# Page order and buffers in a decoder-layer step: keys of the third pair ahead of the first pair's values, a score buffer that pages may share

## The chip, the core and the metric

One core of one Trainium2 chip. The metric is the device time of one execution of the whole program in microseconds. The kernel before took 876.76 us (median of three runs, 876.49 to 877.36).

## What is computed

One decoder layer for 256 prompt tokens and for 8 decode requests of 8 tokens each (64 sample tokens), so 320 tokens stand side by side. Cut to what matters:

```
z = x @ w_in                                  # 2048 -> 8272 columns, all 320 tokens
A: index scores -> top-k keys; sparse attention over 8 heads x 128
   prompt: over its own 256 keys; sample: over 2048 cached keys in 16 pages of 128, and its 8 new keys
   s = q . K[selected] * 128**-0.5 ; p = softmax(s) ; a = p @ V[selected]
B: HGRN2 gated recurrence, 4 heads
M: cross-attention, 4 heads: prompt over 256 memory rows (mk, mv = mem @ w_mem), sample over cached memory
cat = [a, b, m] * silu(gates) ;  y = cat @ w_out ;  x <- LayerNorm(2**0.25 * x + y)
```

The selection is made by a mask: the sample's attention reads all 2048 cached keys and values of every request (`page_table` names the pages), and the mask takes the keys that are not selected out of the softmax. Outputs are the layer's result, the new keys and values, states and memory keys and values.

## The kernel before, in words

**Matmuls.** Inputs are split into a high and a low part in a fast matmul type (xh, xl for activations; wh, wl for weights), and three products (high x high, low x high, high x low) stand for one. A projection block gives 128 columns for 320 tokens (tile pj, matmuls of 128x320); its weights come in two halves of 512 KB, loaded to one of three raw buffers wr, split by ScalarE (wh) and VectorE or GpSimd (wl). `PROJECTIONS` (line 30) lists the order; the memory keys and values (mem: 16 steps, each of a 512 KB weight tile and a 128 KB activation tile) stand late in it, then mq, g3 and g2. After the last projection `split` (line 1474) writes the concatenated branch outputs as high and low parts over xh and xl, and the output projection (pieces named wo) begins.

**Pages.** The sample's attention works on pairs of requests. `PAGES` (line 31) is the order of the page work: K2 are the keys of the third pair, V0 the values of the first, XK and XV the cached memory keys and values. Each K or V entry is eight units, an X entry one unit; a unit reads two tiles of two pages (4 x 512 KB). `unit` (line 657) issues its matmuls, which use the array as four strips of 32 columns. K units write scores to S[p] (a buffer of tag S, 2048 + 64 columns); `soft` (line 1110) adds the mask, takes the exponential and transposes to PTt[p] (one buffer, so it waits until the values of pair p - 1 are done); V units multiply PTt[p] by value pages into the PSUM tile va. The first softmax needs the top-k selection, a long run of VectorE work.

**What sets the order.** Every engine's instructions are put in order when the program is built. `Plan` (line 56) keeps an estimated clock per engine; the main loop (line 1958) steps along it: `loads` (line 1901) issues transfers from SyncE's queue (weights first, then stores, then pages), then come weight splitting, evictions and background generators (`background`, line 1865: index scores, softmax, recurrence, cross-attention, `split`), and at last either page units (`units_now`, line 733) or one quantum of a projection. A visit is one run of page units on TensorE: two units together when both are loaded, one unit alone when the next weights are not about to be ready, or after a wait of 9 us by the plan's clock (`PATIENCE`). On the chip each engine runs its list in order and waits on semaphores.

**Buffers.** `BUFS` (line 236) gives six buffers of tag pg (8 KB per partition) and two of tag S. Pages go to pg; so do other tiles for a time (indexer queries q, relu results more, half of the indexer's cached keys ci, the final LayerNorm's data, the split weights kept for the output projection's last chunk). A page load is issued when a pg buffer is free or about to be, at most two units ahead of the unit that is next, with less than 8 us of transfers outstanding by the plan's clock. `page` (line 637) loads a page's number from SBUF to a register of SyncE just before the transfer that uses it, with bounds given.

```
31   PAGES = ["K0", "K1", "V0", "K2", "V1", "V2", "K3", "XK0", "XK1", "XV0", "XV1", "V3"]
1924 if (half > 46 and n < len(punits) and len(PG) + ("q" in st) + ("more" in st) + ci_live(0) < BUFS["pg"] and n <= nunit + 2
1925         and plan.slot_free("pg", BUFS["pg"]) <= plan.now + 0.2 and plan.t["DMA"] < plan.now + 8):
1926     load_pages(n, b)
```

The record of nearly every instruction goes through one helper (line 154), so that the profile names all of them by that line; groups are told apart by their tiles. The functions that the change touches:

Of the kernel before, what the change touches and what calls it, by code (L numbers as in the profile page):

```python
# [27 lines left out]
PAST = 2048  # L28
HALF = 1032
PROJECTIONS = ["ikw", "iq", "aq", "ak", "av", "b0", "b1", "g0", "b2", "g1", "b3", "mem", "mq", "g3", "g2"]  # L30
PAGES = ["K0", "K1", "V0", "K2", "V1", "V2", "K3", "XK0", "XK1", "XV0", "XV1", "V3"]
# [14 lines left out]
IDLE = 3.0  # L46
TABLES = {AF.Exp: "exp_ln", AF.Ln: "exp_ln", AF.Silu: "silu", AF.Sqrt: "sqrt"}
# [95 lines left out]
class Engine:  # L143
# [3 lines left out]
    def __getattr__(self, op):  # L147
# [3 lines left out]
        def call(*a, **k):  # L151
# [9 lines left out]
            if op == "value_load":  # L161
                plan.t[eng] = max(plan.t[eng], plan.now) + 0.65
            elif op == "dma_start":
                plan.dma(eng, outs[0], ins[0])
            elif op == "indirect_dma_start":
                plan.dma(eng, k["out"], k["in_"])
            elif outs:
                n = max(math.prod(x.shape[1:]) for x in outs + ins)
                plan.run(eng, self.cost(op, outs, ins, n), outs, ins,
                         op in PORT and all(x.space != bass.MemoryType.PSUM for x in outs + ins))  # L170
# [55 lines left out]
def hymba_step(ctx: ExitStack, tc: tile.TileContext, I, O):  # L226
# [9 lines left out]
    BUFS = {"t": 17, "s8": 10, "pg": 6, "bp": 2, "wr": 3, "wh": 4, "wl": 4, "S": 2, "row": 4, "mA": 2, "mB": 2, "pj": 2}  # L236
# [355 lines left out]
    def prep(i, j):  # L592
# [9 lines left out]
        if s.get("res") and kept.index(i) < HOMES:  # L602
            if not spare_w:
                for cols, tag in ((2880, "cat0"), (2240, "cat1"), (2320, "PT"), (2048, "pg"), (2048, "pg")):
                    t = new([128, cols], tag, F32R)
                    plan.split.add(t.tensor.name)
                    spare_w.extend(t[:, 512 * k:512 * k + 512] for k in range(4))
# [29 lines left out]
    def page(e):  # L637
        return SP.value_load(ptab[0:1, e:e + 1], min_val=0, max_val=159)

    def load_pages(n, b):  # L640
        kind, p, u = punits[n]
        t = new([128, 2, 1024], "pg")
        PG[n, b] = t
        for j in range(2):
            if kind in ("XK", "XV"):
                SP.dma_start(t[:, j, :], I["c" + kind][4 * p + 2 * b + j])
            else:
                e = (2 * p + b) * 16 + 2 * u + j
                SP.dma_start(t[:, j, :], I["c" + kind.lower()][bass.ds(page(e), 1)].rearrange("o p c -> p (o c)"))
# [7 lines left out]
    def unit(n):  # L657
        kind, p, u = punits[n]
        tl = [PG.pop((n, b)) for b in range(2)]
        if kind == "K":  # L660
            if u == 0:
                S[p] = new([128, PAST + NS], "S")
            if u % 2 == 0:
# [48 lines left out]
    def unit_ready(n):  # L712
# [3 lines left out]
        if kind == "K":  # L716
            return u % 2 or ("aq", 7) in done and plan.slot_free("kv", 1) <= plan.now and (
                u or plan.slot_free("S", BUFS["S"]) <= plan.now and len(S) + ci_live(1) < BUFS["S"]
# [51 lines left out]
    def ci_live(k):  # L770
        return sum([0, 1, 0, 1][p] == k and ("ci", p) in st for p in range(4))

    def idx_load():
# [3 lines left out]
        for sp in range(2):  # L777
            for p in (2 * sp, 2 * sp + 1):
                st["ci", p] = x = new([128, PAST], ("pg", "S")[p % 2])
# [68 lines left out]
    def idx_sample():  # L848
# [44 lines left out]
        def stack(k):  # L893
# [12 lines left out]
            if (c, f) == (1, 0):  # L906
                del st["ci", 2 * sp + a]
# [202 lines left out]
    def soft(p):  # L1110
# [35 lines left out]
        ACT.copy(PTt[p][:, 16, :], ps)  # L1146
        del S[p]
# [56 lines left out]
    def cross_prompt(h):  # L1204
        yield from wait("mem", ("mq", h), "attn")
        yield from room(4)
# [6 lines left out]
        DVE.tensor_scalar(s8[:, 2:4], s8[:, 0:2], -QS, None, op0=OP.mult)  # L1213
        P = [T(256), T(256)]
        pts = [T(256), T(256)]
        free(MQ.pop(h), st["mkT"][h])
# [12 lines left out]
        free(*P)  # L1229
        for nt in range(2):  # L1230
# [670 lines left out]
    def loads():  # L1901
        nonlocal nw, npg
        while True:
# [20 lines left out]
            if (half > 46 and n < len(punits) and len(PG) + ("q" in st) + ("more" in st) + ci_live(0) < BUFS["pg"] and n <= nunit + 2  # L1924
                    and plan.slot_free("pg", BUFS["pg"]) <= plan.now + 0.2 and plan.t["DMA"] < plan.now + 8):
# [7 lines left out]
            if n == len(punits) and nunit == n and half > n_in - 6 and ("r", 2) not in st:  # L1933
                ln_load(2)
                continue
            return
# [177 lines left out]
```

## Time and profile before

| | us |
|---|---|
| median of three runs | 876.76 |
| the profiled execution, its own time | 878.17 |
| its span, first to last instruction | 876.4 |
| TensorE busy | 860.5 (98%) |
| VectorE busy | 558.0 (64%) |
| ScalarE busy | 423.0 (48%) |
| GpSimd busy | 311.7 (36%) |
| moved by DMA | 266.55 MB, mean 304 GB/s |

How to read it: the profile is one execution. Engines are PE (TensorE), PEld (its weight loads, beside the matmuls), DVE (VectorE), ACT (ScalarE), POOL (GpSimd) and SP (SyncE, which only issues transfers here; SPq is its queue). A group is written `out<-in` with tile names; "x128" counts instructions. A row of the windows gives, for one stretch, the busy microseconds of PE, PEld, DVE, ACT and POOL with counts, then the granted share of TensorE's clock, the busy share of the DMA engines and GB/s. A row of the timeline is start, duration, engine, line, operation, and in brackets the idle time before it and what ended that. A list of waits gives total, number and longest in us. Matmuls are pipelined and their ends are modelled, so the distance between starts tells more than the busy time.

### The profile page before, as it was taken

The numbers are of one execution on the slowest core, as the hardware profiler recorded it, in microseconds if no ns is written. First come the engines' busy times: TensorE is split into PE (matmuls) and PEld (weight loads), VectorE is DVE, ScalarE is ACT, GpSimd is POOL, SyncE is SP. The second block draws the span as 40 slices with busy tenths as digits, with TensorE's granted clock in tenths as the row PEclk, the third lists the DMA queues.
The fourth block names the chain that finished last, engine by engine and source line by source line (L and its number), as shares of the span: only waits on it lengthen the run. The fifth ranks groups of instructions, "written<-read, shape, count | busy, mean of one in ns | idle before, by whom it ended". The sixth has DMA issues, their size and how long they took to land.

```text
span 876.4 us, 19974 instructions
## 1 busy us (share of the span) xinstructions
PE 860.5 (98%) x6972; PEld 730.7 (83%) x6974; DVE 558.0 (64%) x1128; ACT 423.0 (48%) x909; POOL 311.7 (36%) x310
## 2 busy tenths in 40 slices
PE   9999999999999999999999999999999999999996
PEld 8999898878988998879888786777888878788885
DVE  6778989748789984645745563585444333943655
ACT  6445666545463444435545364444444433744432
POOL 0543562255644461322433142334222000613424
PEclk9999999999999999999999999999999999999999
DMA  8555544899999975999999999999998999876633
GB/s 309 182 165 160 158 144 146 300 342 405 362 410 337 372 260 161 339 411 354 398 367 399 412 377 401 405 347 383 325 408 331 350 384 384 295 269 200 192 101 120
DMA packets 84375, 266.55 MB, mean 304 GB/s; under 512 B 10609, under 2 KB 21810, under 8 KB 83634
## 3 DMA queue, kind: packets, MB, share of 16 engines
q1 hardware_dynamic: 83250, 263.18, 81.3%
q0 software_dynamic: 1024, 2.10, 0.8%
q8 instruction: 55, 0.90, 0.4%
q14 instruction: 46, 0.38, 0.1%
HBM read 256.50 MB, written 8.73 MB: 303 GB/s over the span
## 4 chain that ended last, share of the span: by engine, by line
PE 91%; DMA 3%; DVE 2%; ACT 1%; SPq 1%; issue 1%; DVEq 0%; ACTq 0%
PE pj L154 53%; PE mB L154 11%; PE va L154 10%; PE mA L154 9%; PE kv L154 7%; DMA pg<-in_ck 2%; SPq L154 1%; ACT wh L154 1%; DVE wl L154 1%; DMA pg<-in_xT 1%; DVE t L154 1%; DMA wr<-in_wt 0%; DVE pg L154 0%; ACT t L154 0%; DVE cat L154 0%
## 5 line engine op out<-in xcount | busy, mean ns | idle before, releaser
L154 PE MATMUL pj<-xh,wh 128*128 128x320 f32 x1008 | 321.9, 319 | 0.0
L154 PE MATMUL pj<-xh,wl 128*128 128x320 f32 x1008 | 311.5, 309 | 0.0
L154 PE MATMUL pj<-xl,wh 128*128 128x320 f32 x1008 | 311.3, 309 | 0.0
L154 ACT CAST wh<-wr 128x512 fp32r<-128x512 f32 x338 | 205.4, 618 | 210.9 <-PE pj L154 155.3
L154 DVE TENSOR_TENSOR wl<-wr,wh 128x512 fp32r<-128x512 f32 x231 | 178.2, 785 | 183.1 <-ACT wh L154 180.2
L154 POOL TENSOR_TENSOR wl<-wr,wh 128x512 fp32r<-128x512 f32 x107 | 145.2, 1362 | 296.8 <-ACT wh L154 272.9
L154 PEld LDWEIGHTS pj<-xh,wh 128*128 128x128 f32 x1008 | 189.4, 188 | 18.4 <-issue 12.7
L154 PEld LDWEIGHTS pj<-xl,wh 128*128 128x128 f32 x1008 | 189.5, 188 | 1.3
L154 PEld LDWEIGHTS pj<-xh,wl 128*128 128x128 f32 x1008 | 189.2, 188 | 0.0
L154 POOL TENSOR_TENSOR t<-t,t 128x320 f32<-128x320 f32 (+3 forms) x44 | 41.1, 935 | 88.5 <-DVE t L154 41.2
L154 PE MATMUL kv<-pg,qpad 128*32 128x256 f32 x1032 | 62.7, 380 | 3.4 <-DMA pg<-in_ck 3.4
L154 PE MATMUL va<-pg,PT 128*32 128x512 f32 x512 | 59.6, 596 | 0.0
L154 PEld LDWEIGHTS kv<-pg,qpad 128*32 128x32 f32 x1032 | 33.4, 110 | 27.2 <-issue 5.7
L154 PEld LDWEIGHTS va<-pg,PT 128*32 128x32 f32 x512 | 15.1, 109 | 30.5 <-issue 29.3
L154 DVE MAX8 PT<-PT 128x8 f32<-128x1032 f32 x32 | 39.5, 1234 | 0.5
L154 DVE MATCH_REPLACE8 PT<-PT 128x1032 f32<-128x1032 f32 x32 | 39.0, 1217 | 0.0
L154 ACT ACTIVATE t<-t 128x320 f32<-128x320 f32 (+1 forms) x44 | 18.5, 455 | 24.7 <-DVE t L154 24.4
L154 POOL TENSOR_TENSOR t<-t,tabm 128x320 f32<-128x320 f32 x16 | 14.0, 878 | 39.1 <-DVE t L154 35.4
L154 POOL DMA_INDIRECT pg<-in_ci,row x16 | 16.6, 1040 | 26.8 <-DVE row L154 19.9
L154 DVE TENSOR_TENSOR t<-t,t 128x320 f32<-128x320 f32 (+4 forms) x28 | 17.6, 629 | 13.4 <-ACT t L154 6.9
L154 ACT ACTIVATE S<-kv 128x512 f32<-128x512 f32 x16 | 9.6, 598 | 32.6 <-PE kv L154 32.6
L154 PE MATMUL mB<-t,wh 128*128 128x256 f32 x128 | 24.0, 286 | 0.0
(360 smaller groups left out, 1314.1 us busy)
## 6 DMA issues: line engine op xcount, KB each, us to landing
pg<-in_ck SPq DMA_DIRECT2D x128, 512.0 KB
pg<-in_cv SPq DMA_DIRECT2D x128, 512.0 KB
wr<-in_wt SPq DMA_DIRECT2D x126, 512.0 KB
wr<-in_wo SPq DMA_DIRECT2D x36, 512.0 KB
wr<-in_wm SPq DMA_DIRECT2D x16, 512.0 KB
pg<-in_cXK SPq DMA_DIRECT2D x8, 512.0 KB
pg<-in_cXV SPq DMA_DIRECT2D x8, 512.0 KB
pg<-in_xT SPq DMA_DIRECT2D x8, 320.0 KB
```

The source lines that it names most:

```text
L154: res = f(*a, **k)
```

## The change

- `PAGES` becomes K0 K1 K2 V0 V1 K3 V2 V3 XK0 XK1 XV0 XV1: the third pair's keys ahead of the first pair's values, the fourth pair's ahead of the third's values, cross pages last.
- Five pg buffers in place of six, three S buffers in place of two. A page may take an S buffer (`page_tag`): if no pg buffer is free, and if scores that are live, pages that already stand in S, indexer keys, rows of the LayerNorm and key passes that begin up to this unit leave one over. Tiles in S that must not be replaced are pinned in the plan.
- Three of the four indexer key tiles go to S (before: two); one tile of the weights kept for the last output chunk goes to S.
- A page may be loaded up to three units ahead (before: two), with less than 6 us of transfers outstanding (before: 8).
- Page numbers are loaded to registers ahead of time when SyncE has nothing else (`numbers_ahead`), for up to two tiles; bounds are no longer given; the plan counts 0.45 us for one (before: 0.65).
- The prompt's cross-attention no longer waits for four free t buffers; it frees its queries and keys before it takes two buffers, and takes the other two after freeing these.

```diff
--- before.py
+++ after.py
@@ -28,7 +28,7 @@
 PAST = 2048
 HALF = 1032
 PROJECTIONS = ["ikw", "iq", "aq", "ak", "av", "b0", "b1", "g0", "b2", "g1", "b3", "mem", "mq", "g3", "g2"]
-PAGES = ["K0", "K1", "V0", "K2", "V1", "V2", "K3", "XK0", "XK1", "XV0", "XV1", "V3"]
+PAGES = ["K0", "K1", "K2", "V0", "V1", "K3", "V2", "V3", "XK0", "XK1", "XV0", "XV1"]
 DEFER = (0,)
 MIX = [(1, 2), (1, 4), (1, 6), (2, 0)]
 KORDER = (0, 2, 4, 6, 12, 14, 8, 10)
@@ -44,6 +44,7 @@
 HASTE = 2.0
 CALM = 4.0
 IDLE = 3.0
+LOOK = 3
 TABLES = {AF.Exp: "exp_ln", AF.Ln: "exp_ln", AF.Silu: "silu", AF.Sqrt: "sqrt"}
 EXP_LN = 6
 PORT = ("tensor_tensor", "tensor_add", "tensor_sub", "tensor_mul", "scalar_tensor_tensor", "tensor_scalar", "tensor_copy",
@@ -159,7 +160,7 @@
                 outs.append(aps.pop(0))
             ins = aps + ins
             if op == "value_load":
-                plan.t[eng] = max(plan.t[eng], plan.now) + 0.65
+                plan.t[eng] = max(plan.t[eng], plan.now) + 0.45
             elif op == "dma_start":
                 plan.dma(eng, outs[0], ins[0])
             elif op == "indirect_dma_start":
@@ -233,7 +234,7 @@
     ctx.enter_context(tc.manual_schedule())
 
     uid = [0]
-    BUFS = {"t": 17, "s8": 10, "pg": 6, "bp": 2, "wr": 3, "wh": 4, "wl": 4, "S": 2, "row": 4, "mA": 2, "mB": 2, "pj": 2}
+    BUFS = {"t": 17, "s8": 10, "pg": 5, "bp": 2, "wr": 3, "wh": 4, "wl": 4, "S": 3, "row": 4, "mA": 2, "mB": 2, "pj": 2}
 
     def new(shape, tag, dt=F32, p=None):
         uid[0] += 1
@@ -601,7 +602,7 @@
         raw = WR[i][:, w * j:w * j + w]
         if s.get("res") and kept.index(i) < HOMES:
             if not spare_w:
-                for cols, tag in ((2880, "cat0"), (2240, "cat1"), (2320, "PT"), (2048, "pg"), (2048, "pg")):
+                for cols, tag in ((2880, "cat0"), (2240, "cat1"), (2320, "PT"), (2048, "pg"), (2048, "S")):
                     t = new([128, cols], tag, F32R)
                     plan.split.add(t.tensor.name)
                     spare_w.extend(t[:, 512 * k:512 * k + 512] for k in range(4))
@@ -635,18 +636,54 @@
     PG = {}
 
     def page(e):
-        return SP.value_load(ptab[0:1, e:e + 1], min_val=0, max_val=159)
+        return SP.value_load(ptab[0:1, e:e + 1])
+
+    in_s = set()
+
+    def page_tag(n):
+
+        if n > nunit + LOOK:
+            return None
+        if (len(PG) - len(in_s) + ("q" in st) + ("more" in st) + ci_live(0) < BUFS["pg"]
+                and plan.slot_free("pg", BUFS["pg"]) <= plan.now + 0.2):
+            return "pg"
+        ahead = sum(kind == "K" and u == 0 for kind, _, u in punits[nunit:n + 1])
+        if (len(S) + len(in_s) + ci_live(1) + ahead + sum(("r", m) in st for m in range(2)) < BUFS["S"]
+                and plan.slot_free("S", BUFS["S"]) <= plan.now + 0.2):
+            return "S"
+        return None
+
+    numbers = {}
+
+    def number(n, b, j):
+
+        p, u = punits[n][1:]
+        return page((2 * p + b) * 16 + 2 * u + j)
+
+    def numbers_ahead():
+
+        for m in range(npg, npg + 2):
+            n, b = divmod(m, 2)
+            if n < len(punits) and punits[n][0] in "KV":
+                for j in range(2):
+                    if (n, b, j) not in numbers:
+                        numbers[n, b, j] = number(n, b, j)
+                        return
 
     def load_pages(n, b):
         kind, p, u = punits[n]
-        t = new([128, 2, 1024], "pg")
+        tag = page_tag(n)
+        t = new([128, 2, 1024], tag)
         PG[n, b] = t
+        if tag == "S":
+            plan.pinned.add(t.tensor.name)
+            in_s.add((n, b))
         for j in range(2):
             if kind in ("XK", "XV"):
                 SP.dma_start(t[:, j, :], I["c" + kind][4 * p + 2 * b + j])
             else:
-                e = (2 * p + b) * 16 + 2 * u + j
-                SP.dma_start(t[:, j, :], I["c" + kind.lower()][bass.ds(page(e), 1)].rearrange("o p c -> p (o c)"))
+                e = numbers.pop((n, b, j)) if (n, b, j) in numbers else number(n, b, j)
+                SP.dma_start(t[:, j, :], I["c" + kind.lower()][bass.ds(e, 1)].rearrange("o p c -> p (o c)"))
 
     def pair(x, hp):
 
@@ -657,9 +694,12 @@
     def unit(n):
         kind, p, u = punits[n]
         tl = [PG.pop((n, b)) for b in range(2)]
+        plan.pinned.difference_update(t.tensor.name for t in tl)
+        in_s.difference_update([(n, 0), (n, 1)])
         if kind == "K":
             if u == 0:
                 S[p] = new([128, PAST + NS], "S")
+                plan.pinned.add(S[p].tensor.name)
             if u % 2 == 0:
                 st["kv"] = PS([128, 512], "kv")
             c = 256 * (u % 2)
@@ -715,7 +755,7 @@
             return False
         if kind == "K":
             return u % 2 or ("aq", 7) in done and plan.slot_free("kv", 1) <= plan.now and (
-                u or plan.slot_free("S", BUFS["S"]) <= plan.now and len(S) + ci_live(1) < BUFS["S"]
+                u or plan.slot_free("S", BUFS["S"]) <= plan.now and len(S) + len(in_s) + ci_live(1) < BUFS["S"]
                 and (p < BUFS["S"] or ("soft", p - BUFS["S"]) in done))
         if kind == "V":
             return ("soft", p) in done and plan.avail(PTt[p]) <= plan.now and (u < 7 or "attn" in done) and (
@@ -768,7 +808,7 @@
             yield
 
     def ci_live(k):
-        return sum([0, 1, 0, 1][p] == k and ("ci", p) in st for p in range(4))
+        return sum([0, 1, 1, 1][p] == k and ("ci", p) in st for p in range(4))
 
     def idx_load():
 
@@ -776,7 +816,8 @@
         t = -9.0
         for sp in range(2):
             for p in (2 * sp, 2 * sp + 1):
-                st["ci", p] = x = new([128, PAST], ("pg", "S")[p % 2])
+                st["ci", p] = x = new([128, PAST], "S" if p else "pg")
+                plan.pinned.add(x.tensor.name)
                 plan.split.add(x.tensor.name)
             for c in range(2):
                 for f in (1, 0):
@@ -904,6 +945,7 @@
                 ACT.copy(kk[j][own], raw[own])
                 DVE.tensor_sub(kk[j][other], raw[own], kk[j][own].bitcast(F32))
             if (c, f) == (1, 0):
+                plan.pinned.discard(st["ci", 2 * sp + a].tensor.name)
                 del st["ci", 2 * sp + a]
             return kk
 
@@ -1144,6 +1186,7 @@
         ps = PS([128, 128])
         PE.transpose(ps, Sp[:, PAST - 64:], ident)
         ACT.copy(PTt[p][:, 16, :], ps)
+        plan.pinned.discard(S[p].tensor.name)
         del S[p]
         done.add(("soft", p))
 
@@ -1203,7 +1246,6 @@
 
     def cross_prompt(h):
         yield from wait("mem", ("mq", h), "attn")
-        yield from room(4)
         yield need(MQ[h], st["mkT"][h])
         ps = PS([128, 2, 256])
         for tt in range(2):
@@ -1211,9 +1253,8 @@
         s8 = T8()
         DVE.tensor_reduce(s8[:, 0:2], ps, axis=AX.X, op=OP.max)
         DVE.tensor_scalar(s8[:, 2:4], s8[:, 0:2], -QS, None, op0=OP.mult)
+        free(MQ.pop(h), st["mkT"][h])
         P = [T(256), T(256)]
-        pts = [T(256), T(256)]
-        free(MQ.pop(h), st["mkT"][h])
         for tt in range(2):
             ACT.activation(P[tt], ps[:, tt, :], AF.Exp, bias=s8[:, 2 + tt:3 + tt], scale=QS,
                            accum_out=s8[:, 4 + tt:5 + tt])
@@ -1227,6 +1268,7 @@
             for tt in range(2):
                 PE.transpose(pt[:, nt, tt, :], P[tt][:, 128 * nt:128 * nt + 128], ident)
         free(*P)
+        pts = [T(256), T(256)]
         for nt in range(2):
             ACT.copy(pts[nt], pt[:, nt].rearrange("p a b -> p (a b)"))
         yield need(*pts)
@@ -1921,8 +1963,7 @@
                 SP.dma_start(dst, src)
                 continue
             n, b = divmod(npg, 2)
-            if (half > 46 and n < len(punits) and len(PG) + ("q" in st) + ("more" in st) + ci_live(0) < BUFS["pg"] and n <= nunit + 2
-                    and plan.slot_free("pg", BUFS["pg"]) <= plan.now + 0.2 and plan.t["DMA"] < plan.now + 8):
+            if half > 46 and n < len(punits) and page_tag(n) and plan.t["DMA"] < plan.now + 6:
                 load_pages(n, b)
                 npg += 1
                 continue
@@ -1933,6 +1974,8 @@
             if n == len(punits) and nunit == n and half > n_in - 6 and ("r", 2) not in st:
                 ln_load(2)
                 continue
+            if half > 40 and plan.t["SP"] <= plan.now:
+                numbers_ahead()
             return
 
     def prep_ready(i, j):
```

## The prediction

> **What bounds the kernel now.** I read the page first, then the waits of TensorE, then the stages by windows, then the places that the change touches.
>
> ```profile
> span 876.4 us, 19974 instructions
> ...
> PE 860.5 (98%) x6972; PEld 730.7 (83%) x6974; DVE 558.0 (64%) x1128; ACT 423.0 (48%) x909; POOL 311.7 (36%) x310
> ...
> L154 PE MATMUL kv<-pg,qpad 128*32 128x256 f32 x1032 | 62.7, 380 | 3.4 <-DMA pg<-in_ck 3.4
> ...
> L154 ACT ACTIVATE S<-kv 128x512 f32<-128x512 f32 x16 | 9.6, 598 | 32.6 <-PE kv L154 32.6
> ...
> pg<-in_ck SPq DMA_DIRECT2D x128, 512.0 KB
> ```
>
> TensorE is busy for 860.5 of 876.4 us, so nothing that the other engines do is worth anything unless TensorE waits for it. Its 16 us of idle time are all that an edit which leaves the matmuls alone can win, with the price of switching the array between its shapes. The only group with idle time worth the name is the key matmuls, which wait for pages.
>
> ```profile
> PE kv L154 <- DMA pg<-in_ck: 3.4, 4, 1.6
> PE pj L154 <- issue: 1.4, 1, 1.4
> PE kv L1789 <- DVE t L154: 1.1, 1, 1.1
> ```
>
> Four waits for key pages, one of 1.4 us that the profile cannot name, and the start. Everything else is below half a microsecond. The windows tell in which stage pages are late:
>
> ```profile
> 240.00:260.00 20.00, 20.00 (x180) 17.96 (x179) 15.60 (x28) 11.69 (x30) 10.99 (x9) 1.00 1.03 410
> 300.00:320.00 20.00, 20.00 (x149) 19.58 (x142) 19.55 (x19) 8.65 (x18) 13.63 (x8) 1.00 0.93 345
> 320.00:340.00 20.00, 19.98 (x140) 18.75 (x139) 13.17 (x35) 12.14 (x22) 5.84 (x5) 1.00 0.41 117
> 340.00:360.00 20.00, 20.00 (x152) 15.40 (x154) 10.00 (x13) 7.53 (x16) 1.29 (x1) 1.00 0.86 311
> 600.00:620.00 20.00, 18.75 (x304) 15.37 (x303) 7.96 (x22) 8.89 (x25) 4.48 (x5) 1.00 1.03 401
> 620.00:640.00 20.00, 18.11 (x173) 15.27 (x171) 7.83 (x16) 9.22 (x25) 6.91 (x6) 1.00 0.90 321
> ```
>
> The last two numbers of a row are the busy share of the DMA engines and GB/s. From 600 to 640 us the transfers run full and TensorE is short of work by 3.1 us; from 320 to 340 us TensorE is full and the transfers run at 117 GB/s. SyncE's issues show why:
>
> ```profile
> 307.45 1.43 SPq L154 DMA_DIRECT2D pg<-in_cv  x2
> ...
> 345.45 0.34 SPq L154 DMA_DIRECT2D pg<-in_cv  x1
> ```
>
> All six page buffers hold values of the first pair by 309 us, and those can't be used before the first softmax. No page is asked for in 36.6 us. That is the hole that the third pair's keys go into.
>
> **The change part by part.**
>
> *Keys in the hole.* Keys need no softmax, only a score buffer. At 410 GB/s the three windows from 300 to 360 us could carry (65 + 293 + 99) GB/s x 20 us = 9.1 MB more. A visit (two units) reads 8 pages of 512 KB, 4.2 MB, so that is 2.2 visits, at most. In the stretch where pages set the pace the visits stand so:
>
> ```profile
> 436.06 3.59 PE kv L154 x64
> 439.65 10.76 PE pj L154 x72
> ```
>
> One visit in 14.35 us. The page stream comes to lead by about two visits, 29 us. The matmuls are the same ones, moved; the scores' evictions on ScalarE (598 ns each, four for the pair) move into a window where ScalarE has 8.65 of 20 us of work, so I cost them at nothing; without that cover they would be 2.4 us. The projections that filled the hole move back behind the keys.
>
> [...]
>
> *Page waits.* The idle column understates them, since a waiting matmul's modelled end runs on. The starts say more:
>
> ```profile
> 595.57 0.63 PE L154 MATMUL kv<-pg,qpad 128*32 128x256 f32 x4
> 596.78 1.92 PE L154 MATMUL kv<-pg,qpad 128*32 128x256 f32 x28 [0.58 <-DMA pg<-in_ck]
> ...
> 603.03 0.63 PE L154 MATMUL kv<-pg,qpad 128*32 128x256 f32 x4
> 604.19 1.07 PE L154 MATMUL kv<-pg,qpad 128*32 128x256 f32 x16 [0.53 <-DMA pg<-in_ck]
> ...
> 612.54 0.41 PE L154 MATMUL kv<-pg,qpad 128*32 128x256 f32 x2
> 613.67 1.07 PE L154 MATMUL kv<-pg,qpad 128*32 128x256 f32 x16 [0.72 <-DMA pg<-in_ck]
> ...
> 631.97 1.93 PE L154 MATMUL kv<-pg,qpad 128*32 128x256 f32 x32
> ...
> 634.85 0.62 PE L154 MATMUL kv<-pg,qpad 128*32 128x256 f32 x4
> 637.05 1.92 PE L154 MATMUL kv<-pg,qpad 128*32 128x256 f32 x28 [1.57 <-DMA pg<-in_ck]
> ...
> 655.05 3.66 PE L154 MATMUL kv<-pg,qpad 128*32 128x256 f32 x64
> ```
>
> Four matmuls need 3.59/16 = 0.22 us; so the waits cost 596.78 - 595.57 - 0.22 = 0.99, then 0.94, about 1.0 (the pair at 612.54 is half a group) and 1.98: 4.9 us. All are the fourth pair's keys, read as they land in the stage where memory weights and pages share the transfers. In the new order those keys come two visits earlier and stand mostly ahead of that stage; what stands in it are the third pair's values. Does the wait pass on to them? The nearest rows are the same pair's values in the first half of that stage now:
>
> ```profile
> 558.51 1.92 PE L154 MATMUL va<-pg,PT 128*32 128x512 f32 x16
> 560.69 1.90 PE L154 MATMUL va<-pg,PT 128*32 128x512 f32 x16
> ```
>
> They show no wait. But values that follow keys directly are read as they land, too. Ends: -4.9 us (all gone), 0 (all passed on), +4.9 (twice as many, since eight units may wait where four do). I take three of four gone, -3.7 us, nearer to the rows of values.
>
> *Broken pairs.* The fourth pair's keys take seven visits (587.5, 595.6, 603.0, 612.5, 632.0, 634.9, 655.1) instead of four. A visit turns the array into four column strips and back. Back costs 10.76 us less 72 matmuls at the spacing of the long row below, 0.147, so 0.2 us; the way in is 746.29 - 746.05 - 0.147 = 0.1 us.
>
> ```profile
> 20.06 14.82 PE pj L154 x101
> ...
> 587.48 1.86 PE kv L154 x32
> ```
>
> Three visits fewer at 0.3 us are -0.9 us. Ends: 0 (the values break up as the keys did) and -1.5 us (two broken pairs elsewhere also close).
>
> *Cross pages last.* Today the fourth pair's last values stand at the seam between the last projection and the output projection:
>
> ```profile
> 746.05 0.31 PE L154 MATMUL pj<-xh,wl 128*128 128x320 f32 x1
> 746.29 3.64 PE L154 MATMUL va<-pg,PT 128*32 128x512 f32 x32
> ...
> 750.72 0.50 PE L154 MATMUL mA<-wh,xh 128*128 128x512 f32 x1
> ```
> ```profile
> 746.78 1.63 ACT L154 CAST xh<-cat 128x256 fp32r<-128x256 f32 x5
> ```
> ```profile
> 747.25 2.69 POOL L154 TENSOR_TENSOR xl<-cat,xh 128x256 fp32r<-128x256 f32 x3 [30.69 <-ACT xh L154]
> ```
>
> The output projection needs xh and xl, and they overwrite what the last projection reads. The first high part comes at 746.78, its low part from 747.25 takes 2.69/3 = 0.9 us, so the first output matmul could start at about 748.2. The last values run from 746.29 to 750.72 and hide all of that. With pages two visits ahead, the last page unit stands some 29 us before the last projection, nothing lies over the seam, and TensorE waits 748.2 - 746.2 = 2.0 us. Ends: 0 (a visit still stands there) and 2.5 us. I take +1.8, since VectorE may make the first low part a little sooner.
>
> The clock stays out of this sum: the two rows from 600 to 640 us show 1.00 with a wait of 2 us in them. [...]
>
> *Five page buffers, a third score buffer.* A page load may now take a score buffer that the next keys need, or wait for one, and behind it on SyncE's queue stand the weight loads. While three pairs' scores live there are five tiles for pages, a pair needs four, and the fifth lands during the visit (3.59 us). Cost 0 so long as projections fill TensorE; ends -0.5 and +2 us, a wait of the 637 us size.
>
> *Page numbers ahead.* It frees SyncE, not TensorE:
>
> ```profile
> 590.75 3.72 SPq L154 DMA_DIRECT2D pg<-in_ck  x4
> 594.57 0.38 SPq L154 DMA_DIRECT2D wr<-in_wm  x1
> ```
>
> Four page issues take 3.72 us where bare ones would take about 1.5 (0.38 each), so a weight load behind them goes out up to 2.2 us sooner. The transfers are full then, so it lands hardly sooner: 0, with -1 us as the better end. The planner's constants (lookahead, backlog, the cost of a number) only place the same work. The prompt's cross-attention loses a wait for four buffers, and frees two before it takes two: 0. The indexer's keys move from page buffers to score buffers ahead of the first scores, when those are not yet wanted: 0.
>
> Sum: -3.7 - 0.9 + 1.8 = -2.8 us. The profiled execution took 878.17 us, 1.4 more than the median of the runs, 876.76; I take the difference over to the median: 876.76 - 2.8 = 874.0 us.
>
> **The rivals.** *The seam stays covered and all waits go.* If the softmax of one pair holds back the next values (values of two pairs now follow each other twice), the lead melts and cross pages are still there at the last projection. Then -4.9 - 0.9 = -5.8, 871.0 us. For it: the last cross values need the cross softmax and come a visit after the cross keys. Against it: a lead of 29 us.
>
> *The waits pass on.* The stage of memory weights starves whatever unit stands in it; 0 for the waits, -0.9 for pairs, +1.8 for the seam: +0.9, 877.7 us. For it: 401 GB/s at a share of 1.03 leaves no room there, and the change takes no byte out of that stage.
>
> *Slower: eight single value units wait in that stage.* Today four of seven key visits waited, 1.2 us each. If the third pair's values come singly and all eight units wait so, that is 9.8 us where 4.9 were: +4.9, no pairs won, +1.8 for the seam: +6.7, 883.5 us. It decides from about six such waits on (6 x 1.2 = 7.2; 7.2 - 4.9 - 0.9 + 1.8 = +3.2). Against it: the values' rows at 558 us.
>
> **How the numbers follow.** A change of 0.2%, 1.75 us, is about what a measurement of this kernel can tell from none. Chances: forecast 0.45, covered seam 0.2, waits passed on 0.2, slower 0.15. Of the forecast's case three quarters lie beyond 1.75 us: faster 0.34 + 0.2, about 0.54. Same: the other quarter, 0.11, and 0.14 of the waits passed on: 0.25. Slower: 0.06 + 0.15: 0.21. The range goes from 870.0 (the covered seam, with 1 us for the queue) to 878.5 (waits passed on, with a seam of 2.5); it leaves out the slower case and a little below.
>
> **What would show it.** Right: no hole in page issues from 309 to 345 us, third keys there; fewer than two waits for pages in TensorE's list; four visits rather than seven for the fourth pair's keys; the last page unit well before the last projection; a gap of about 2 us between that and the first output matmul. Wrong: waits of value matmuls for value pages between 560 and 640 us, a visit across the seam, or new waits before 540 us, where there are none now.

## The result and the profile after

| | before | after |
|---|---|---|
| median of six runs, us | 877.03 (876.49 to 878.01) | 882.15 (880.89 to 885.2) |
| the profiled execution, us | 878.17 | 880.89 |
| its span, us | 876.4 | 879.1 |
| mean granted clock, all runs | 0.997 to 0.998 | 0.993 to 0.998 |

The change made the kernel slower: ratio 1.0063, 95% interval 1.0046 to 1.0080. The forecast was 874.0 (870.0 to 878.5), with 0.21 for slower. The page of the changed kernel, its first lines and the key matmuls:

```profile
span 879.1 us, 19324 instructions
...
PE 859.7 (98%) x6974; PEld 729.6 (83%) x6974; DVE 555.0 (63%) x1137; ACT 424.1 (48%) x909; POOL 301.6 (34%) x301
...
L155 PE MATMUL kv<-pg,qpad 128*32 128x256 f32 x852 | 58.0, 380 | 0.0
```

TensorE does the same work (two matmul records more, 0.8 us less busy) and the key matmuls, the group that waited for pages before, now wait for nothing: the 852 of this row read page buffers, the rest read score buffers. Yet the span is 2.7 us longer. SyncE's issues show that the hole in the page stream is gone; keys (in_ck) go out where nothing did:

```profile
316.08 0.86 SPq L155 DMA_DIRECT2D pg<-in_ck  x2
...
326.32 5.47 SPq L155 DMA_DIRECT2D pg<-in_ck  x8
...
338.17 1.37 SPq L155 DMA_DIRECT2D S<-in_ck  x2
```

So the change does what it says. What it costs stands in the waits of TensorE (total, times, longest):

```profile
PE mB L155 <- ACT t L155: 2.8, 1, 2.8
PE mA L155 <- DVE cat L155: 1.5, 2, 1.2
PE mA L155 <- DVE wl L155: 1.5, 1, 1.5
PE pj L155 <- issue: 1.1, 1, 1.1
...
PE mA L155 <- ACT xh L155: 0.9, 1, 0.9
PE pj L155 <- DVE t L155: 0.8, 1, 0.8
PE mA L155 <- POOL xl L155: 0.5, 1, 0.5
...
PE va L155 <- DMA pg<-in_cv: 0.3, 1, 0.3
```

Before, the list began with four waits for pages. Now it has one of 0.3 us, and above it stand waits for ScalarE, VectorE and GpSimd, engines that are 34 to 63% busy. TensorE's own rows say where:

```profile
41.79 0.93 PE L155 MATMUL mA<-t,t 64*128 64x128 f32 x8 [1.21 <-DVE cat L155]
...
620.46 1.03 PE L155 MATMUL mA<-ident,S 128*128 128x128 f32 x8
624.27 0.33 PE L155 MATMUL mB<-ident,S 128*128 128x128 f32 x1 [2.77 <-ACT t L155]
...
750.08 0.31 PE L155 MATMUL pj<-xh,wl 128*128 128x320 f32 x1
...
751.26 0.51 PE L155 MATMUL mA<-wh,xh 128*128 128x512 f32 x1 [0.87 <-ACT xh L155]
...
752.26 0.50 PE L155 MATMUL mA<-wh,xl 128*128 128x512 f32 x1 [0.50 <-POOL xl L155]
...
765.15 0.50 PE L155 MATMUL mA<-wl,xh 128*128 128x512 f32 x1 [1.51 <-DVE wl L155]
```

Measured from start to start, as the prediction did with the page waits, each place loses its idle time and a little more: 1.3 us at 41.8 (the same matmuls waited 0.17 before, which isn't taken off here), 2.9 at 624.3, 1.8 at the seam (1.0 and 0.8), 1.7 at 765.2, and 1.2, 1.0 and 0.8 at three smaller ones (650.6, 572.9 and 554.0): 10.7 us. Gone are the page waits of 4.9 us, the unnamed wait of the old kernel (1.6), 0.5 at 624.9, and 0.6 for two stretches fewer in which the array stands in another shape than 128x128 (58 in place of 60, 0.3 each by the prediction's estimate). The difference is +3.1 us, beside +2.7 between the two profiled executions. The medians lie 5.1 us apart, since the profiled execution lies 1.1 above its median before and 1.3 below it after.

**The largest wait: the fourth pair's softmax at 624 us.** The softmax needs 17 transposes of the score tile S. Sixteen of them go to bank mA here. The last one goes to bank mB and finds there the memory keys, whose last product was issued at 620.3. Of VectorE and then ScalarE, which empty that bank together, and of GpSimd beside them:

```profile
621.53 1.34 DVE L155 TENSOR_TENSOR wl<-wr,wh 128x512 fp32r<-128x512 f32 x1 [0.35 <-PE mA L155]
622.80 0.68 DVE L155 COPY PT<-mA 128x512 f32<-128x512 f32 x1
623.40 0.74 DVE L155 COPY t<-mB 128x256 f32<-128x256 f32 x2
```
```profile
621.39 0.59 ACT L155 COPY PT<-mA 128x512 f32<-128x512 f32 x1
623.84 0.70 ACT L155 COPY t<-mB 128x256 f32<-128x256 f32 x2 [1.86 <-DVE t L155]
```
```profile
621.06 1.27 POOL L155 TENSOR_TENSOR wl<-wr,wh 128x512 fp32r<-128x512 f32 x1 [2.10 <-ACT wh L155]
```

VectorE's copy out of mB (623.40) stands behind a weight split and behind the softmax's own copy out of mA; ScalarE's stands behind VectorE's. The copies are short. They are late because the softmax arrives in the microsecond in which the memory keys end, while the splits go on. The split on VectorE is itself slow, 1.34 us where the one before it took 0.69: it begins inside GpSimd's split and ends 0.55 us after it (the last section has more on this).

In the old order the fourth pair's keys came behind the third pair's values. They ended at 659 us and the softmax's transposes into mB came at 666, long after the last memory product (610.7). Now these keys stand ahead of the third pair's values and end at 542. Their transposes still have to wait for those values, since PTt is one buffer, and the last of those values stand here:

```profile
614.29 1.04 PE L155 MATMUL va<-avS,PT 128*32 128x512 f32 x8
```

The transposes begin right behind them, at 615.3, and so the softmax meets the end of the memory keys.

**The late weights at 765 us.** VectorE makes a share of the low parts of x. In the old profile its last such step begins at 754.4 us, 3.7 after the first output matmul; here low parts are still made 12 us after the first output matmul, ahead of the split in question:

```profile
761.29 1.53 DVE L155 TENSOR_TENSOR xl<-cat,xh 128x256 fp32r<-128x256 f32 x1
...
763.56 0.41 DVE L155 TENSOR_TENSOR xl<-cat,xh 128x256 fp32r<-128x256 f32 x1
763.89 1.21 DVE L155 TENSOR_TENSOR wl<-wr,wh 128x512 fp32r<-128x512 f32 x1
```

The weight split that TensorE waits for starts only when those are done.

### The profile page after: what moved, and what is told of

It reads as the page before. It is cut to its first block, busy times and chain, and to the rows that moved or that the text cites. A ratio compares the mean times of both kernels' runs of the same rounds, so it can differ in the third digit from the quotient of the medians.

```text
span 879.1 us, 19324 instructions
## 1 busy us (share of the span) xinstructions
PE 859.7 (98%) x6974; PEld 729.6 (83%) x6974; DVE 555.0 (63%) x1137; ACT 424.1 (48%) x909; POOL 301.6 (34%) x301
## 5 line engine op out<-in xcount | busy, mean ns | idle before, releaser
L155 DVE TENSOR_TENSOR wl<-wr,wh 128x512 fp32r<-128x512 f32 x233 | 176.2, 769 | 182.0 <-ACT wh L155 178.0
L155 POOL TENSOR_TENSOR wl<-wr,wh 128x512 fp32r<-128x512 f32 x105 | 138.6, 1323 | 301.9 <-ACT wh L155 229.3
L155 PE MATMUL kv<-pg,qpad 128*32 128x256 f32 x852 | 58.0, 380 | 0.0
L155 PEld LDWEIGHTS kv<-pg,qpad 128*32 128x32 f32 x852 | 30.5, 110 | 20.3 <-issue 1.6
L155 POOL DMA_INDIRECT S<-in_ci,row x24 | 24.8, 1035 | 30.1 <-DVE row L155 22.7
L155 DVE TENSOR_TENSOR t<-t,t 128x320 f32<-128x320 f32 (+3 forms) x30 | 17.0, 568 | 11.2 <-POOL t L155 6.2
```

The costliest lines, as they stand in the source:

```text
L155: res = f(*a, **k)
```

## The experiments

Theory A, after the result: the page part of the forecast holds, and the loss is made of new waits at three places, the fourth pair's softmax, the uncovered seam with the late weights behind it, and the early index scores; undoing them one by one gives the time back. Rival B: the new order, or the buffer counts, costs in itself, spread over the kernel. The order of all engines is made by a planner that sees every edit, so an edit at one place shifts others; hence each run is read by its waits as well as by its time. Ratios are against the kernel before, run on the same chip.

### The seam covered by holding the cross values: e1_seam, e6_seam_pages

`unit_ready` may give the cross values only when the last projection has been issued:

```diff
-        return p or ("attn" in done and all(
+        return p or ("lastT" in done and "attn" in done and all(
```

> The changed kernel with one edit: the two cross value units may only start once the last projection has been issued, so that they stand over the seam to the output projection. Theory A (the loss is a handful of separate waits that the new order makes: 1.8 us at the seam, 2.9 us where the fourth pair's softmax transposes wait for the memory keys' evictions, 1.7 us for a low weight part at 765 us, 1.3 us at 42 us): the two waits at 751 us go, 1.8 us less than the changed kernel's 882.15, about 880.3, and the granted clock of its runs stays as uneven as before (0.993 to 0.998). Theory B (the waits are only where a general lack shows, late weights behind pages on the transfer queue, and move when one place is mended): within 1 us of 882.

Measured: 888.77 us, ratio 1.0133 (1.0116 to 1.0151). Much worse than either theory gave, but not by its matmuls. SyncE's queue and ScalarE at the seam:

```profile
748.01 0.33 SPq L155 DMA_DIRECT2D S<-in_xn  x1
748.43 9.50 SPq L155 DMA_DIRECT2D wr<-in_wo  x5
```
```profile
754.35 2.42 ACT L155 CAST wh<-wr 128x512 fp32r<-128x512 f32 x4 [14.46 <-DMA wr<-in_wo]
```

The residual rows (in_xn) are loaded to a score buffer, and the held cross pages now sat in score buffers too. The load of these rows waits 17.9 us for the cross values and goes out at 748.01, and the output weights queued behind it on SyncE go out only then; ScalarE stood 14.46 us for them, and TensorE 7.5. As a test of the seam this run says nothing; as a test of sharing buffers it says much. The next version keeps the cross values out of the score buffers:

```diff
             return "pg"
+        if punits[n][0] == "XV":
+            return None
         ahead = sum(kind == "K" and u == 0 for kind, _, u in punits[nunit:n + 1])
```

(a cut of `page_tag`; the edit of e1_seam is in this run too).

> The changed kernel with the two cross value units held to the last projection, as in the first of these runs, but with their pages kept out of the score buffers, so that the residual rows' load need not wait for them on the transfer queue in front of the output weights. Theory A (the first try lost 7.5 us because the rows' load stood in front of the output weights): the output weights are split before the seam, the cross values cover it, the two waits of 1.8 us go: about 880 us. Theory B: the output weights are late again (they are held by raw buffers or by the cross values' own order), 886 or more.

Measured: 878.18 us, ratio 1.0017 (1.0008 to 1.0026), 4.0 less than the changed kernel and 2 less than theory A gave. TensorE at its seam:

```profile
746.17 1.92 PE L155 MATMUL va<-pg,t 128*32 128x512 f32 x16
747.91 1.90 PE L155 MATMUL kv<-pg,t 128*32 128x512 f32 x16
749.74 0.50 PE L155 MATMUL mA<-wh,xh 128*128 128x512 f32 x1
```

No brackets: the first output matmul waits for nothing, and from 744 to 780 us nothing waits at all, at 765 either. The seam (1.8) and the late weights (1.7) are 3.5 of the 4.0 us. Both go with this pair of edits. It isn't shown that the uncovered seam makes the late weights: e9_uncovered and e8_old_order, below, have the seam's two gaps and no wait for weights behind them.

### The seam of the old kernel uncovered: e9_uncovered

The kernel before, with the matmuls of the last projection weights held until all page units are done:

```diff
-        if i not in WH:
+        if i not in WH or i == last_T and nunit < len(punits):
```

> The kernel before with one edit: the second half of the last projection may only start when all page units are done, so that the last values stand ahead of it and nothing lies over the seam. Theory A (an uncovered seam is the largest part of what the change lost: its two first waits, and the low weight part that is late 14 us on because the split starts later against the output weights; covering it won 4.0 us in the changed kernel): 3 to 4.5 us slower than the kernel before, 880 to 881.5, with waits for xh and xl at the seam. Theory C (the cover won 4.0 us there for another reason, as where the cross values stood): the two first waits alone, 1.8 us, or nothing.

Measured: 878.76 us, ratio 1.0019 (1.0010 to 1.0028): 2.0 more. TensorE at the seam:

```profile
749.80 0.50 PE L154 MATMUL mA<-wh,xh 128*128 128x512 f32 x1 [0.87 <-ACT xh L154]
750.81 0.50 PE L154 MATMUL mA<-wh,xl 128*128 128x512 f32 x1 [0.50 <-POOL xl L154]
```

The same two gaps as in the changed kernel, 1.8 us from start to start, and no wait for weights behind them. That is what theory C gave; the 3 to 4.5 of theory A was too much. The 2.0 of the medians can't be read as the seam's price: the waits for key pages fall from 3.4 us to 1.3 at the same time, and the two profiled executions differ by -0.6 us (877.54 and 878.17). The gaps are the cleaner reading.

### The softmax of the fourth pair: e2_soft_after_mem, e3_both, e5_soft_lag, e10_seam_pause

The first three hold the softmax back. e2_soft_after_mem does so until the memory products are out of mB, e3_both adds the edit of e1_seam, and e5_soft_lag asks that the memory keys have landed 3 us before:

```diff
+        while held["mB"] == 2 and "mem" not in done:
+            yield
+        if "mem" in done and p == 3:
+            yield need(*st["mkT"], lag=3.0)
```

(the first two lines in all three, the last two in e5_soft_lag alone).

> The changed kernel with one edit: a pair's softmax transposes are not begun while the memory products hold both mB banks. Theory A: the 2.8 us wait at 624 us goes, 2.9 us less; and if that idle stretch is what lowers the granted clock in most runs (0.993 to 0.996 against 0.998 in the profiled one), the clock is 0.998 in every run, which is worth another 1.5 to 2.5 us at the median: 877 to 879 us. Without the link to the clock: 879.3 with clocks as uneven as now. Theory B: the wait comes back nearby, within 1 us of 882.

> Both edits, the covered seam and the softmax transposes held back. Theory A: 1.8 + 2.9 us less and the clock at 0.998: 875 to 877 us, at or under the kernel before (877.0). Theory B: 880 or more.

> The changed kernel with one edit: the fourth pair's softmax transposes wait until the memory keys' evictions are 3 us old by the planner's clock (before this, holding them back to the end of the memory products left 2.1 us of the wait). Theory A (separate waits, and idle stretches of two to three microseconds cost a stretch at half clock behind them): no wait of the transposes for the memory keys' evictions; 2.9 us less than the changed kernel and fewer half-clock stretches, 877.5 to 880 us, clocks 0.997 to 0.998 in most runs. Theory B (the waits show a general lack and move): 881 to 883 us.

Measured: 881.28 (1.0055, 1.0041 to 1.0070), 888.40 (1.0122, 1.0104 to 1.0140) and 880.83 (1.0045, 1.0032 to 1.0059). The holding moves the wait and doesn't remove it. Theory A missed in all three; the time of e5_soft_lag lies between its two theories. In e5_soft_lag the same kind of row still leads the list:

```profile
PE mB L155 <- ACT t L155: 2.0, 1, 2.0
```

It now stands before the recurrence's transposes at 626.5 us, since whoever needs bank mB next must wait for the memory keys' eviction. The eviction, not the softmax, is what is late: the last memory product is issued at 621.6 there, and the two engines copy it out from 625.4 and 626.1. e3_both is told with its clock, below.

e10_seam_pause takes e6_seam_pages and instead holds other work back, the recurrence's decay steps on GpSimd, VectorE and ScalarE, while the memory products end:

```diff
             for li in range(-2, 6):
+                while last_mem - 1 <= half and wspec[half]["kind"] != "wo" and "mem" not in done:
+                    yield
```

> The changed kernel with the seam covered (878.2), and the recurrence's decay steps held back from the last memory product until the memory keys are evicted. Theory A (the wait of 2.8 us at 625 us is for the eviction of the memory keys, and that is late because it is queued behind decay steps on VectorE and ScalarE, which wait for GpSimd): the wait goes, 2.5 to 3 us less, 875 to 876 us, clocks nearer to 0.998. Theory D (the eviction is late by itself, or the recurrence, held back, is late elsewhere): 877.5 or more.

Measured: 874.35 us, ratio 0.9964 (0.9951 to 0.9977), 3.8 less than e6_seam_pages. The row for the eviction of mB is gone from the list, whose top is now:

```profile
PE mA L155 <- DVE cat L155: 1.5, 2, 1.2
PE kv L1835 <- DVE t L155: 1.1, 1, 1.1
PE pj L155 <- DVE t L155: 0.5, 1, 0.5
```

What went with it is not only the decay steps: the planner now sets the softmax's transposes between 615.2 and 621.8 us, ahead of and among the last memory products and all into mA, so that nobody asks for mB while it is being emptied. The eviction also comes sooner: VectorE's copy begins 1.3 us after the last product is issued (622.96 and 621.69), where it began 3.1 us after it in the changed kernel (623.40 and 620.34). The collision is avoided; which step's delay made it isn't separated. The wait was 2.9 us of the 3.8. The rest isn't taken apart: the waits for value pages fall from 0.8 to 0.2 us, and the clock may have a part, since e6_seam_pages ran at 0.995 to 0.998 and this one at 0.997 to 0.998.

### Order, counts and sharing apart: e4_order_only, e7_buffers_only, e8_old_order

e4_order_only is the kernel before with the new `PAGES`, five page and three score buffers and the spare weight tile in S, without sharing. e7_buffers_only is the same without the new order. e8_old_order is the changed kernel with the old `PAGES`.

```diff
-PAGES = ["K0", "K1", "K2", "V0", "V1", "K3", "V2", "V3", "XK0", "XK1", "XV0", "XV1"]
+PAGES = ["K0", "K1", "V0", "K2", "V1", "V2", "K3", "XK0", "XK1", "XV0", "XV1", "V3"]
```

> The kernel before with the new page order alone, with five page and three score buffers, which that order needs; pages stay in page buffers, no numbers ahead, lookahead and backlog as before. Theory A: the seam (1.8 us) and, if the fourth pair's softmax again falls on the end of the memory products, the 2.9 us are there too, while the fourth pair's keys no longer wait (4.9 us less): 875 to 880 us. Theory B (sharing and numbers ahead are what costs): at least 3 us under the changed kernel, with neither wait in the list.

> The kernel before with five page buffers and three score buffers, page order as before, no sharing, no numbers ahead. Theory A (the 1.2 us wait at 42 us belongs to the buffer counts, since it stood in the run with the order alone as well; fewer page tiles starve visits): that wait is there, 1.3 us; page waits grow; 878 to 882 us. Theory B (it belongs to the order): no wait at 42 us, 877 to 878 us.

> The changed kernel with the page order of before; sharing, buffer counts and numbers ahead as changed. Theory A (the order brings the seam and the clash with the memory keys, sharing and numbers cost nothing of their own): the fourth pair's values stand at the seam again, no wait there, no wait of transposes at the end of the memory products; the fourth pair's keys wait for pages again: 876 to 879 us. Theory B (sharing and numbers are what costs): 881 or more.

Measured: 889.82 (1.0145, 1.0129 to 1.0160), 888.01 (1.0121, 1.0105 to 1.0136) and 881.85 (1.0054, 1.0041 to 1.0068). The first two lie above what any theory gave for them (875 to 882), though the wait at 42 us stands in e7_buffers_only's list as its theory A said. For e8_old_order theory A expected a time near the kernel before and waits for the fourth pair's keys, and both missed. Two rows of its list show a part of why:

```profile
PE mA L155 <- ACT xh L155: 0.9, 1, 0.9
...
PE mA L155 <- POOL xl L155: 0.5, 1, 0.5
```

Its seam is uncovered too. With the rest of the change in place the pages end early in the old order as well (the last values start at 739.96, the last projection matmul at 751.81), so it is the lead and not the place of V3 that uncovers it. Nor does its list have a wait for pages: the page waits end without the new order, by the other parts of the change. It has no wait for a copy out of mB; its waits are others, of 1.5 us and less each. The new counts by themselves cost 11 us (e7_buffers_only), and sharing, lookahead, early numbers and the smaller edits win 6 of them back in the old order (888.01 to 881.85). On top of that the new order changes nothing that these runs can tell, 881.85 to 882.15. Part of rival B stands, then: the counts cost, over many small waits. Parts can't be added up in this kernel: the counts alone cost more than the whole change.

### The early wait and all edits together: e11_seam_memset, e12_seam_all

The wait at 41.8 us is for `cat`, made on VectorE. In the changed kernel VectorE, then GpSimd beside it:

```profile
36.37 1.66 DVE L155 CAST row<-rows 128x2 int32<-128x2 f32 x1
...
36.45 2.00 DVE L155 STREAM_SHUFFLE t<-pj 128x320 f32<-128x320 f32 x1
```
```profile
36.54 0.96 POOL L155 MEMSET avS<- 64x1024 f32 x1
```

In the old kernel the two VectorE steps, and the memset of avS, which ends 0.1 us after the first of them begins:

```profile
36.17 0.62 DVE L154 CAST row<-rows 128x2 int32<-128x2 f32 x1
...
36.24 0.97 DVE L154 STREAM_SHUFFLE t<-pj 128x320 f32<-128x320 f32 x1
```
```profile
35.28 0.98 POOL L154 MEMSET avS<- 64x1024 f32 x1
```

The cast's end goes with the memset's: it comes 0.53 us after it in both kernels (38.03 after 37.50, 36.79 after 36.26), and the same cast takes 0.16 us at 42.26 in the changed kernel, where no GpSimd instruction is under way. The shuffle isn't slower by itself. It ends 0.42 us after the cast in both, and its row counts the time in which it stands behind the cast. e11_seam_memset takes e6_seam_pages and moves this memset behind a later projection:

```diff
         POOL.memset(st["qpad"], 0.0)
+        yield from wait(("iq", 4))
         POOL.memset(avS[0:64], 0.0)
```

> The changed kernel with the seam covered, and the clearing of the new values' tile on GpSimd moved from behind the first query block to behind the fifth; TensorE's list is the same, instruction for instruction. Theory A (VectorE's copy of row numbers at 36 us takes 1.7 us instead of 0.6 because GpSimd's memset runs beside it, and the 1.2 us wait at 42 us comes of that): the wait shrinks by about 1 us, 877.2 us. Theory E (it comes of the page transfers' order): 878.2 as before.

Measured: 877.53 us, ratio 1.0008 (0.9999 to 1.0017), 0.65 less than e6_seam_pages (the two intervals overlap), and the wait for cat at 42 us falls from 1.2 us to 0.3, as theory A said. The order of TensorE's work is the same in both. The cast there stands ahead of a weight split and meets the memset of qpad instead: it takes 2.05 us and again ends 0.53 us after that memset (37.58 after 37.05). The shuffle's row falls to 1.20 us. e12_seam_all has all edits: covered seam, pause and memset.

> All three edits on the changed kernel: seam covered, decay steps held back, memset later. Theory A: the sum of the two, 874 to 875.5 us, under the kernel before (877.0) by 0.2% or more. Theories D and E: 877 or more.

Measured: 874.06 us, ratio 0.9964 (0.9952 to 0.9977), beside 876.76 for the kernel before. It beats the kernel before by 2.7 us and the changed kernel by 8.1. The top of its list:

```profile
PE kv L155 <- DMA pg<-in_ck: 1.6, 1, 1.6
PE pj L155 <- DVE t L155: 1.4, 1, 1.4
PE kv L1835 <- DVE t L155: 1.1, 1, 1.1
PE mA L155 <- DVE cat L155: 0.7, 2, 0.3
```

## Why the prediction was wrong

**What held.** The hole is filled, the page waits fall from 4.9 us to about 0.8, the fourth pair's keys take four visits instead of seven (492 to 542 us) without a wait, 117 us earlier for the last visit (538.4 and 655.1) where I had said two visits, the pages lead at the end by about 40 us (the last cross values start at 710.5, the last projection matmul at 750.1) where 29 were worked out, and the seam costs 1.81 us where +1.8 was taken. The three terms of the sum were -3.7, -0.9 and +1.8; they measured about -4.1, -0.6 and +1.8. By these waits that part alone would have come out at -2.9. The runs give the new order less: with everything else in place it changes the median by 0.3 us (e8_old_order, 881.85, and the changed kernel, 882.15), and e8_old_order has lost the page waits too.

**What failed.** The step that failed is the costing of everything else at nothing: "Cost 0 so long as projections fill TensorE; ends -0.5 and +2 us" for the buffers, and 0 for what moved on the other engines. Measured start to start that term is about +8 us (10.7 of new losses less 1.8 of the seam and the 0.8 of a page wait that is counted above), with 2.1 gone elsewhere (1.6 and 0.5): -2.9 + 8.1 - 2.1 = +3.1. Measured by runs, the buffer counts alone cost 11 us in the old order (888.01 beside 876.97), and with everything but the new order 4.9 us (881.85). The wait for cat of 1.2 us comes with the counts: e7_buffers_only has it without the new order, the sharing or the move of the indexer's keys. The largest single wait, 2.9 us, comes from the fourth pair's keys and its softmax standing earlier: I asked whether the values around it would wait for pages, and never what the softmax would meet on bank mB and on VectorE's queue. That engines are idle by half says little for a wait of 2 us in which three short steps stand in line.

**The seam was right in size and short in reach.** I priced the first output matmul alone. Behind it low parts of x were still being made when the output weights had to be split, and another 1.7 us went there. The two edits of e6_seam_pages take both away; that the seam alone brings the second isn't shown, since e9_uncovered has the first without it.

**The clock was left out of the sum, and should not have been.** The changed kernel's runs go from 880.89 us at a granted clock of 0.998 to 885.2 at 0.993; the kernel before stays at 0.997 to 0.998. Windows of 4 us around the two long waits of e3_both, the clock third from the end:

```profile
624.00:628.00 4.00, 2.01 (x15) 1.75 (x14) 2.56 (x7) 1.96 (x5) 3.19 (x7) 0.94 0.95 303
628.00:632.00 4.00, 4.00 (x21) 4.00 (x20) 1.05 (x2) 2.00 (x4) 1.29 (x1) 0.64 0.92 303
...
754.00:758.00 4.00, 0.00 (x0) 0.00 (x0) 1.42 (x3) 1.92 (x4) 0.00 (x0) 0.50 0.92 371
758.00:762.00 4.00, 2.98 (x6) 2.09 (x7) 3.85 (x7) 4.00 (x13) 2.77 (x3) 0.50 0.65 192
```

Behind a wait of 2.0 us (4.00 - 2.01 in the first row) the clock falls: (1 - 0.94) x 4 + (1 - 0.64) x 4 = 1.7 us are lost, a stretch of 3.4 us if the clock stood at 0.50 in it, as it does from 754 to 762. The prediction left the clock out because a wait of that size showed 1.00 in the kernel before; the same size did cost clock here.

A longer wait gave both outcomes. Windows with the wait of 2.8 us at 624, of the changed kernel and then of e11_seam_memset:

```profile
620.00:624.00 4.00, 1.50 (x14) 1.26 (x12) 3.16 (x5) 2.14 (x5) 2.94 (x5) 1.00 0.98 362
624.00:628.00 4.00, 3.73 (x26) 3.73 (x27) 1.18 (x3) 2.05 (x6) 0.78 (x2) 1.00 0.98 335
628.00:632.00 4.00, 4.00 (x30) 3.81 (x29) 2.02 (x6) 1.60 (x3) 1.94 (x2) 1.00 0.97 365
```
```profile
620.00:624.00 4.00, 2.47 (x22) 2.23 (x20) 2.52 (x4) 2.96 (x7) 1.97 (x2) 1.00 1.01 369
624.00:628.00 4.00, 2.77 (x11) 2.77 (x12) 1.46 (x4) 1.59 (x5) 1.74 (x5) 0.62 1.00 340
628.00:632.00 4.00, 4.00 (x29) 4.00 (x28) 1.75 (x6) 1.24 (x2) 0.89 (x1) 0.96 0.97 338
```

TensorE is idle for 2.8 us in each. The changed kernel keeps 1.00; e11_seam_memset loses (1 - 0.62) x 4 + (1 - 0.96) x 4 = 1.7 us. So a wait of 2 to 3 us cost its length alone in one execution and 1.7 us more in two others, and what decides between the two isn't shown. This fits the median of the changed kernel, 1.3 above its profiled execution; its other runs left no trace, so where each lost clock isn't shown either.

**The rivals.** Of the slower one nothing came but the sign: no value unit waits between 560 and 640 us. Of the signs of being wrong, a new wait before 540 us came, the one at 41.8. "The waits pass on" is nearest in effect, with the difference that they pass to evictions and splits, not to pages. The covered seam was the right wish: made by hand (e6_seam_pages) it gave 878.2 where 871.0 was worked out, since the other new waits were still there; with these treated as well, 874.1.

**Not settled.** The waits that the profile calls "issue" (1.1 us here, 1.4 before). Which of the steps queued ahead of mB's eviction makes it late, since the pause shifts the softmax too. Why five page buffers without sharing cost 11 us was not taken apart: the waits of 0.2 us and more in its trace come to 11.3 us, those of the old kernel to 7.2, so they hold some 4 of the 11. e12_seam_all with the old page order was not tried, so how much of its gain is the order's stays open.

## What to carry to other kernels

When a block of matmuls is moved, price the two seams that it leaves and the neighbours that it brings together, by the evictions and splits that are queued there in the microsecond of the meeting, and not by the average load of the engines. A transfer lead that is won can uncover work that the late transfer was hiding (1.8 us at the seam here): hold something back to cover the seam. Before letting a held tile live in a shared buffer, look at what the transfer queue has behind the next load to that buffer.

## What the hardware showed that was not expected

**VectorE's steps took longer beside GpSimd's.** I had counted the two engines as independent. The 128x2 cast that takes 0.16 us with GpSimd idle (at 42.26 in the changed kernel) took 1.66 us beside GpSimd's memset of avS and 2.05 us beside that of qpad. In five traces (before, changed, e7_buffers_only, e11_seam_memset, e12_seam_all) it ended 0.53 to 0.54 us after the end of the one of them that stood beside it. VectorE's weight splits show the same beside GpSimd's arithmetic. In the changed kernel 174 of the 233 splits begin while no GpSimd instruction is under way, and none of these takes more than 0.69 us. Another 46 begin inside a GpSimd TENSOR_TENSOR; their median is 1.08 us, the longest takes 1.76, and all end 0.55 to 0.68 us after it. The split that stands ahead of the eviction at 624 us (1.34 us) and the late one at 765 us (1.21) are two of these. A split there that began inside a memset, at 35.76, took 0.69.

**The clock fell after a short wait.** In e3_both it stood at 0.94 and 0.64 in the two windows from 624 to 632 us, behind a wait of 2.0 us, and 1.7 us went with it.
